# A token shift by one row: 112 + 15 + 1 rows of both halves in three transfers instead of 127 + 127 + 1

## The chip, the cores and the metric

The kernel runs on one core of a Trainium2 chip. Its time is the device time of one execution in microseconds (us). TensorE (PE) has two clock levels, 1.2 and 2.4 GHz, and the profile gives the granted clock as a share of the higher one.

## The reference

Two blocks of a transformer run one after the other on 256 tokens of width 1024, batch 1. The first block has two layers (windowed attention with a dense feed-forward, then attention with forgetting and a mixture of 8 experts). The second block mixes three branches: a recurrence of the RWKV-7 kind, a block attention and a state space model. A mixture of 32 experts follows. The change touches one step of the recurrence. Its input `z` is the projection of each token onto 1792 columns, and each token is blended with the token before it, the first token with zero:

```
z = x @ w_in[:, :1792]                    # 256 tokens x 1792
shifted = concat([zeros(1), z[:-1]])      # by one token
z = z + (shifted - z) * mu                # mu: one number per column
```

## The kernel before

Tokens lie on the 128 partitions in two halves, so `rz` is a tile of [128, 2, 1792]: partition p of half `tb` is token 128*tb + p. A shift by one token is a move by one partition, which compute engines don't do here; it is done with transfers from SBUF to SBUF into the tile `rzp`.

The projection is computed in four chunks of columns, in the order `ZCHUNKS = ((1536, 256), (512, 512), (0, 512), (1024, 512))`. For each, `gemm` multiplies for both halves, and each half's result is copied from PSUM to `rz` by ScalarE (ACT, L310) or VectorE (DVE, L312). Then `shift` is started for the chunk. Its first part clears row 0 of `rzp` on GpSimd (POOL, L1867), issues the transfers on SyncE (SP: L1869 twice, 127 rows of each half; L1870, the row that goes from the last token of the first half to the first row of the second), and loads the chunk's `mu` (tile `rmu`, L1883). Its second part (`tensor_sub`, POOL L1873 for half 0, DVE L1874 for half 1) and third part (L1877, L1878) stand in the program inside the next chunk's multiplications. Those of the last chunk stand inside the first gate's, `gate(2, m)`. The tile `rzp` has one buffer, so a chunk's transfers wait until the chunk before is blended.

Every engine works its own list in the order in which the program was recorded. `weave` recorded this order by an estimate of the time on PE, and it is the same in both kernels. So an instruction that waits holds all that stand behind it on its engine. SP issues the transfers above and also the weight loads: `wr` tiles (L107), each issued when a buffer is free, that is after a `wr` was split into high and low parts `ws` by ACT (L123) and DVE (L124). Then come the recurrence's constants: `rk_k`, `rk_a` and others, loaded by `begin` right behind the last chunk's `rmu`.

Names used below: the transposes through PE of `sq` (L222) belong to the state space branch, and their input is made by DVE L1790 and L1792. The transposes of `rz` (L222) begin the recurrence (`early`), after ACT L1914 and L1915. `early` then multiplies the keys by `rk_k` (DVE L1932) and takes exponentials (ACT L1942 to L1944). L2415 on DVE and L2416 on ACT are the gate's bias and sigmoid. Behind this stage follow the recurrence itself, the last projections, and the mixture of 32 experts, whose weights are loaded through the same `wr` buffers.

Of the kernel before, what the change touches and what calls it, by code (L numbers as in the profile page):

```python
# [1809 lines left out]
class Rwkv:  # L1810
# [51 lines left out]
    def shift(self, ep, c, w):  # L1862

        k, nc, z = self.k, self.k.nc, self.z
        cs = slice(c, c + w)
        zp = ep.tile([128, 2, 512], F32, name="rzp", tag="rzp", bufs=1)
        nc.gpsimd.memset(zp[0:1, 0, :w], 0.0)  # L1867
        for tb in range(2):
            nc.sync.dma_start(zp[1:128, tb, :w], z[0:127, tb, cs])  # L1869
        nc.sync.dma_start(zp[0:1, 1, :w], z[127:128, 0, cs])  # L1870
        mu = self.rowload(ep, "rwkv_mu_2", 512, "rmu", c)
        yield
        nc.gpsimd.tensor_sub(zp[:, 0, :w], zp[:, 0, :w], z[:, 0, cs])  # L1873
        nc.vector.tensor_sub(zp[:, 1, :w], zp[:, 1, :w], z[:, 1, cs])  # L1874
        yield
        for tb, e in ((1, nc.vector), (0, nc.gpsimd)):
            e.tensor_mul(zp[:, tb, :w], zp[:, tb, :w], mu[:, :w])  # L1877
            e.tensor_add(z[:, tb, cs], z[:, tb, cs], zp[:, tb, :w])  # L1878
# [934 lines left out]
```

## Time and profile before

| | |
|---|---|
| time, median of 3 runs (lowest to highest) | 1944.18 us (1944.09 to 1948.15) |
| the profiled execution's own time | 1946.39 us |
| its span, first to last instruction | 1944.7 us |
| PE busy | 1763.3 us, 91% |
| DVE, ACT, POOL busy | 709.1, 450.3, 375.5 us |
| mean granted clock | 0.958 |

The times in views count from the span's start. What lies around the span in the profiled execution is 1946.39 - 1944.7 = 1.7 us. A row of a timeline gives start, duration, engine, line, operation and tiles; in brackets the engine's idle time before it and what ended it. `SPq` rows are issues of transfers: their duration is the time that SP took to issue, not that of the transfer.

### The profile page before, as it was taken

The page shows a single profiled execution, that of the slowest core. Times are in us where ns is not written, and L with a number is a line of the kernel's source. Part 1 is how long each engine was busy: PE and PEld are TensorE (multiplying, and loading weights), DVE is VectorE, ACT ScalarE, POOL GpSimd, SP SyncE. Part 2 cuts the span into 40 slices and gives each one's busy share as a digit, 9 for nine tenths or more (in the row PEclk, how much of TensorE's full clock was granted, in tenths as well). Part 3 has the DMA queues.
Part 4 walks back from the last instruction along what each step waited for, and adds up shares of the span by engine and source line. Part 5 has one row for each costly group of instructions (what it writes and reads, how often), then busy time and mean ns, then how long its engine had stood idle before and what let it go on. Part 6 is the DMA issues. An engine that isn't in the chain of part 4 may idle for free. (4 is left out here: it accounts for less than half of the span.)

```text
span 1944.7 us, 41930 instructions
## 1 busy us (share of the span) xinstructions
PE 1763.3 (91%) x18587; PEld 1200.5 (62%) x18587; DVE 709.1 (36%) x1081; ACT 450.3 (23%) x785; POOL 375.5 (19%) x636
## 2 busy tenths in 40 slices
PE   8989999899699999999999999899637989889886
PEld 7867888797546555454545354588526767766552
DVE  5658655554401202020202020457517565621102
ACT  5534443353200000000000100043214333211101
POOL 5411999111100000000000000163114142000001
PEclk9999999899899999999999999899878999989998
DMA  6515665545399999999999799465224233899997
GB/s 217 161 63 186 215 213 194 158 120 215 127 388 386 385 398 376 410 369 408 375 405 379 284 422 423 154 210 164 85 83 153 78 93 121 315 355 408 409 408 302
DMA packets 138588, 515.99 MB, mean 265 GB/s; under 512 B 22248, under 2 KB 51350, under 8 KB 112800
## 3 DMA queue, kind: packets, MB, share of 16 engines
q1 hardware_dynamic: 135120, 497.39, 68.1%
q0 software_dynamic: 3280, 15.83, 2.4%
q8 instruction: 149, 2.44, 0.5%
q14 instruction: 39, 0.32, 0.1%
HBM read 503.48 MB, written 7.87 MB: 263 GB/s over the span
## 5 line engine op out<-in xcount | busy, mean ns | idle before, releaser
L218 PE MATMUL bank_r<-wl,gx 128*32 128x352 f32 x6144 | 462.2, 462 | 7.6 <-DMA wl<-in_w_exp_in_dram 5.2
L218 PE MATMUL bank_g<-ws,xh 128*128 128x256 f32 (+2 forms) x1440 | 388.4, 350 | 11.6 <-DVE ws L124 4.1
L218 PEld LDWEIGHTS bank_r<-wl,gx 128*32 128x32 f32 x6144 | 205.4, 111 | 257.9 <-issue 220.5
L124 DVE TENSOR_TENSOR ws<-wr,ws 128x1024 fp32r<-128x1024 f32 (+1 forms) x200 | 258.1, 1302 | 210.6 <-ACT ws L123 210.4
L218 PEld LDWEIGHTS bank_g<-ws,xh 128*128 128x128 f32 x1440 | 257.4, 195 | 50.5 <-issue 7.0
L123 ACT ACTIVATE ws<-wr 128x1024 fp32r<-128x1024 f32 (+1 forms) x200 | 209.3, 1057 | 171.6 <-PE bank_g L218 107.8
L218 PE MATMUL bank_g<-ws,xl 128*128 128x256 f32 (+2 forms) x720 | 235.9, 343 | 4.3 <-DVE xl L341 4.3
L218 PE MATMUL bank_r<-wl,ehT 128*32 128x256 f32 x4224 | 230.0, 379 | 1.7 <-DVE ehT L1400 1.5
L1399 DVE TENSOR_TENSOR eh<-eh,bank_r 128x352 f32<-128x352 f32 x48 | 22.9, 505 | 535.6 <-PE bank_r L218 535.1
L218 PEld LDWEIGHTS bank_r<-wl,ehT 128*32 128x32 f32 x4224 | 139.8, 110 | 91.0 <-issue 5.5
L533 POOL TENSOR_SCALAR lnmv<-lnmv 128x1 f32<-128x1 f32 x10 | 7.7, 771 | 823.7 <-DVE lnmv L532 823.7
L218 PEld LDWEIGHTS bank_g<-ws,xl 128*128 128x128 f32 x720 | 140.9, 196 | 18.9 <-DVE xl L341 5.8
L1420 ACT COPY ey<-bank_r 128x256 f32<-128x256 f32 x24 | 8.9, 372 | 456.7 <-PE bank_r L218 456.1
L218 PE MATMUL bank_g<-wr,xgx 128*32 128x256 f32 x864 | 65.6, 388 | 19.3 <-DMA wr<-in_expert_w_up_dram 7.0
L1391 ACT ACTIVATE eh<-bank_r 128x352 f32<-128x352 f32 x48 | 22.2, 464 | 206.7 <-PE bank_r L218 201.6
L218 PEld LDWEIGHTS bank_t<-xOH,x 128*128 128x128 f32 x256 | 61.7, 336 | 3.8 <-issue 2.9
L218 PE MATMUL bank_t<-xOH,x 128*128 128x128 f32 x256 | 63.2, 409 | 0.9 <-DVE xOH L2586 0.9
L218 PEld LDWEIGHTS bank_g<-wr,xgx 128*32 128x32 f32 x864 | 30.5, 111 | 53.9 <-DMA wr<-in_expert_w_up_dram 12.8
L615 POOL TENSOR_TENSOR aP<-aP,ast 128x512 f32<-128x512 f32 (+1 forms) x20 | 24.8, 1242 | 174.9 <-DVE ast L613 133.7
L218 PE MATMUL bank_g<-ws,hh 128*128 128x512 f32 x176 | 57.5, 399 | 0.0
L218 PE MATMUL bank_g<-ws,oh 128*128 128x512 f32 x128 | 44.6, 411 | 0.0
L1400 DVE STREAM_TRANSPOSE ehT<-eh 128x704 f32<-128x704 f32 x24 | 43.0, 1791 | 0.8
(698 smaller groups left out, 2102.0 us busy)
## 6 DMA issues: line engine op xcount, KB each, us to landing
wl<-in_w_exp_in_dram SPq DMA_DIRECT2D x128, 1408.0 KB, 9.0
wl<-in_w_exp_out_dram SPq DMA_DIRECT2D x64, 1408.0 KB, 8.9
wr<-in_expert_w_gate_dram SPq DMA_DIRECT2D x56, 512.0 KB, 10.2
wr<-in_w_in_dram SPq DMA_DIRECT2D x54, 512.0 KB, 4.1
wr<-in_expert_w_down_dram SPq DMA_DIRECT2D x54, 512.0 KB, 10.2
wr<-in_expert_w_up_dram SPq DMA_DIRECT2D x52, 512.0 KB, 10.2
wr<-in_w_ffn_in_dram SPq DMA_DIRECT2D x44, 512.0 KB, 4.1
wr<-in_w_out_dram SPq DMA_DIRECT2D x24, 512.0 KB, 4.4
```

Source lines behind the costliest of these rows:

```text
L123: nc.scalar.activation(hv, v, AF.Copy)
L124: nc.vector.tensor_sub(lv, v, hv.bitcast(F32))
L218: self.nc.tensor.matmul(out, lhsT, rhs, start=start, stop=stop)
L533: nc.gpsimd.tensor_scalar(mv[:, 2:3], mv[:, 1:2], 1e-5, None, op0=OP.add)
L615: e.tensor_mul(P[:, hs, :nk], P[:, hs, :nk], st[:, 3, hs].rearrange("p (h o) -> p h o", o=1).to_broadcast([128, 2, nk]))
L1391: nc.scalar.activation(h[:, g, s * H2:s * H2 + H2], pa[g][s], AF.Silu)
L1399: nc.vector.tensor_mul(v, v, pb[g][s])
L1400: nc.vector.transpose(hT[:, g], h[:, g].rearrange("p (r j) -> p j r", j=KF))
L1420: nc.scalar.copy(y[:, g], ps[g])
```

## The change

The two transfers of 127 rows, one for each half, become one of 112 rows of both halves and one of 15 rows of both halves. The single row stays as it is.

```
-        for tb in range(2):
-            nc.sync.dma_start(zp[1:128, tb, :w], z[0:127, tb, cs])
+        nc.sync.dma_start(zp[1:113, :, :w], z[0:112, :, cs])
+        nc.sync.dma_start(zp[113:128, :, :w], z[112:127, :, cs])
         nc.sync.dma_start(zp[0:1, 1, :w], z[127:128, 0, cs])
```

The lists of PE, DVE, ACT and POOL are the same in both programs. Only SP's differs, at four places. This is the third and fourth of them: the chunks of columns 0 and 1024. Each row is one issue; the numbers at its end are the pattern of the transfer (rows first), and x2 stands for two rows alike.

```order
 L107 DMA wr_13338<-in_w_in_dram 128x2x512
 L107 DMA wr_13361<-in_w_in_dram 128x2x512
-L1869 DMA rzp<-rz 127x512 x2
+L1868 DMA rzp<-rz 112x2x512
+L1869 DMA rzp<-rz 15x2x512
 L1870 DMA rzp<-rz 1x16x32
 L1883 DMA rmu<-in_rwkv_mu_dram 128x512
 L107 DMA wr_13437<-in_w_in_dram 128x2x512
 L107 DMA wr_13456<-in_w_in_dram 128x2x512
```

Two transfers by halves became two by rows, at the same place in SP's list; nothing moved past another load. Behind the last chunk's `rmu` SP's list goes on with the recurrence's constants, as before (rows of the changed program):

```order
 L1883 DMA rmu<-in_rwkv_mu_dram 128x512
 L1883 DMA rk_k<-in_rwkv_k_k_dram 128x512
 L1883 DMA rk_a<-in_rwkv_k_a_dram 128x512
 L1883 DMA rr_k<-in_rwkv_r_k_dram 128x512
 L1883 DMA rln_w<-in_rwkv_ln_w_dram 128x512
```

These rows moved against nothing: the single row's transfer and `rmu` stand ahead of them in both programs.

## Rows read from the trace of the kernel before

**Rows 1.** The page: span, then PE's busy tenths in 40 slices.
```profile
span 1944.7 us, 41930 instructions
...
PE   8989999899699999999999999899637989889886
```

**Rows 2.** PE's timeline, 1358 to 1475 us: its four rows with long idle time.
```profile
1363.65 1.22 PE L218 MATMUL bank_g<-ws,xh 128*128 128x512 f32 x2 [4.05 <-DVE ws L124]
...
1397.38 2.09 PE L222 MATMUL bank_t<-ident,sq 128*128 128x128 f32 x8 [14.22 <-DVE sq L1792]
...
1429.80 0.66 PE L222 MATMUL bank_t<-ident,rz 128*128 128x128 f32 x2 [15.95 <-DVE rz L312]
...
1467.44 1.87 PE L218 MATMUL bank_t<-rind,ru 128*128 128x2 f32 x8 [22.63 <-ACT ru L1943]
```

**Rows 3.** DVE's timeline, 1381 to 1464 us.
```profile
1381.50 1.23 DVE L124 TENSOR_TENSOR ws<-wr,ws 128x1024 fp32r<-128x1024 f32 x1 [1.65 <-ACT ws L123]
1393.46 0.69 DVE L1874 TENSOR_TENSOR rzp<-rzp,rz 128x512 f32<-128x512 f32 x1 [10.74 <-DMA rzp<-rz]
...
1397.15 0.41 DVE L1790 TENSOR_SCALAR st<-st 128x512 f32<-128x512 f32 x1
1397.60 0.69 DVE L1792 TENSOR_TENSOR sq<-hsv,st 128x512 f32<-128x512 f32 x1
...
1426.16 0.69 DVE L1874 TENSOR_TENSOR rzp<-rzp,rz 128x512 f32<-128x512 f32 x1 [18.11 <-DMA rzp<-rz]
...
1428.97 0.68 DVE L312 COPY rz<-bank_g 128x512 f32<-128x512 f32 x1
...
1458.60 1.18 DVE L1932 TENSOR_TENSOR ru<-rz,rk_k 128x512 f32<-128x512 f32 x1 [22.22 <-DMA rk_k<-in_rwkv_k_k_dram]
...
1463.65 0.68 DVE L2415 TENSOR_TENSOR hm<-bank_g,hgb 128x512 f32<-128x512 f32 x1
```

**Rows 4.** SP's timeline at the chunks of columns 512, 0 and 1024.
```profile
1367.39 5.50 SPq L1869 DMA_DIRECT2D rzp<-rz  x2
1372.93 10.17 SPq L1870 DMA_DIRECT2D rzp<-rz  x1
...
1401.42 4.83 SPq L1869 DMA_DIRECT2D rzp<-rz  x2
...
1431.52 6.16 SPq L1869 DMA_DIRECT2D rzp<-rz  x2
1437.73 10.30 SPq L1870 DMA_DIRECT2D rzp<-rz  x1
...
1448.70 0.42 SPq L1883 DMA_DIRECT2D rk_k<-in_rwkv_k_k_dram  x1
```

**Rows 5.** Stretches: length, busy us of PE to POOL, PE clock, DMA share, GB/s.
```profile
1363.60:1369.20 5.60, 5.55 (x34) 4.92 (x34) 4.82 (x7) 1.17 (x2) 1.09 (x2) 0.71 0.67 190
...
1397.30:1401.00 3.70, 3.62 (x13) 3.00 (x14) 3.63 (x6) 2.09 (x3) 0.00 (x0) 0.51 0.14 14
...
1429.80:1434.00 4.20, 4.20 (x10) 2.68 (x12) 4.17 (x5) 0.00 (x0) 1.50 (x3) 0.50 0.56 149
...
1441.50:1444.90 3.40, 3.30 (x11) 1.70 (x9) 0.00 (x0) 0.00 (x0) 0.00 (x0) 1.00 0.06 24
...
1467.40:1471.00 3.60, 3.56 (x12) 3.20 (x13) 0.00 (x0) 3.55 (x4) 1.55 (x2) 0.50 0.06 24
```

**Rows 6.** Issue to landing, min/median/max: `wr` from w_in, 1300 to 1480 us; `hgb`.
```profile
DMA to landing us min/median/max: 3.6/5.8/12.1
...
DMA to landing us min/median/max: 3.4/3.7/6.8
```

**Rows 7.** ACT's timeline around the first piece of `early`.
```profile
1414.17 0.31 ACT L1915 ACTIVATE rz<-rz 128x128 f32<-128x128 f32 x1
```

**Rows 8.** A stretch behind the stage, columns as in rows 5.
```profile
1590.00:1620.00 30.00, 30.00 (x489) 23.87 (x486) 15.46 (x20) 7.29 (x9) 9.33 (x8) 1.00 0.35 104
```

**Rows 9.** SP's own waits, 1640 to 1680 us: in total, times, longest.
```profile
SPq L107 <- DVE ws L124: 28.0, 12, 10.9
```

## The prediction

> **What bounds the kernel now.** I read the page's slices first. PE is busy at nine tenths or nearly so almost everywhere, but two slices next to each other, about 1361 to 1458 us, show 6 and 3 tenths, and the slice behind them 7 [rows 1]. That is where the four chunks are shifted. Next I read PE's timeline there. Four waits stand out: 4.05 us, 14.22, 15.95 and 22.63 [rows 2]. The first is not ended by a shift: DVE had other work ahead of the split of a weight. The other three make 52.8 us, and they are the change's field.
>
> Next I read DVE's timeline to see what held it [rows 3]. It sat idle 10.74 us and 18.11 us ahead of L1874, both ended by the landing of `rzp`, and 22.22 us ahead of L1932, ended by the landing of `rk_k`. Then SP: issuing the two half transfers took it 5.5 us and the single row 10.17 us in the chunk of columns 512, and 6.16 and 10.30 us in that of columns 1024. `rk_k`, which waits for no computed value, was issued only at 1448.70 [rows 4]. The stretches say why: from 1441.5 to 1444.9, with a half transfer under way, the DMA share is 0.06, one engine of 16, at 24 GB/s [rows 5]. A half of 127 rows of 2 KB is 260,096 bytes; at 24 GB/s that is 10.8 us, and two of them 21.7. This fits: the first issue at 1367.39 and DVE's start at 1393.46 lie 26.1 us apart [rows 3, 4]. So now the two halves go one after the other through a single DMA engine, and SP can't issue past them.
>
> **The change part by part.** Removed: eight transfers of 127 rows. Added: four of 112 rows and four of 15 rows, both halves in each. I expect the 112 rows to be spread over 16 engines, as 128 rows of a `wr` are. Nearest rows for the landing: `hgb`, 256 KB, 3.4 to 6.8 us (median 3.7), and the `wr`s of this stretch, 512 KB, 3.6 to 12.1 us (median 5.8), the long ones behind the half transfers [rows 6]. The 15 rows are 61,440 bytes, at one engine's 24 GB/s 2.6 us, and less on more engines. I take 5 us from a chunk's first issue to the last landing; bounds 3.4 and 12.1 + 2.6 = 14.7. SP's issues I take at 0.6 us each. One more issue per shift is then 0.6 us on SP, in time that SP spends waiting now: no cost. One wait is moved: the first transfer now needs both halves' copies. DVE's or ACT's second copy was there before the second issue anyway, and SP's list has nothing else between the two, so I cost that at nothing; should it matter, it is the few us by which the first half started earlier.
>
> The Trainium skill speaks to the spread ("DMA: Bandwidth & Descriptors", section "Why a DMA increments its semaphore by 16 and not by 1"): a transfer uses the largest number of engines up to 16 that divides the count of its slowest dimension, hence 1 for 127. By it 112 rows use 16 and 15 rows use 15. The trace agrees for 127 (share 0.06) [rows 5]; no run here shows the other two.
>
> First shift that counts, columns 512. PE stops at 1397.38 - 14.22 = 1383.16 [rows 2] for transposes of `sq`, whose input DVE makes behind L1874. DVE was free at 1381.50 + 1.23 = 1382.73 [rows 3]. In the new kernel SP issues from 1367.4 as before and the rows lie in `rzp` by 1372.4 (1382.1 at the upper bound), so DVE goes on at 1382.7. L1874 0.69, L1790 0.41, L1792 0.69 [rows 3] end at 1384.5. PE then waits 1.4 us instead of 14.2: 12.8 saved. What is late next is DVE's own work.
>
> Second, columns 0. All that follows is 12.8 us earlier. SP's first issue moves from 1401.42 to 1388.6 [rows 4], landing by 1393.6. DVE reaches L1874 at 1426.16 - 18.11 = 1408.05 before [rows 3], now at 1395.3: no wait. Behind it stand L1874, one split and the copy L312, 0.69 + 1.2 + 0.68, ready by 1398 or, if the split waits for ACT, 1399. PE has work until 1429.80 - 15.95 = 1413.85 before, now 1401.05, so L312 is no longer late. Next in line is ACT: the transposes also read what L1915 writes, at 1414.48 before [rows 7], now 1401.7. I leave 1 us of 15.95: 15.0 saved, 27.8 in all.
>
> Third, columns 1024 and the constants. SP's first issue moves from 1431.52 to 1403.7 [rows 4]. Three issues and `rmu` at 0.6 us, then `rk_k` goes out at about 1406.2 and lands 3.7 to 5.8 us later, say at 1411.5. DVE is ready for L1932 at 1458.60 - 22.22 - 27.8 = 1408.6, so it waits 3 us and not 22. L1932 0.7, two splits of 1.2 and L1874 0.7 follow; L2415 starts at 1415.3. From L2415 to PE's next matmul it took 1467.44 - 1463.65 = 3.8 us (a sigmoid, a table load and two exponentials on ACT) [rows 2, 3]: 1419.1. PE runs out of work at 1467.44 - 22.63 - 27.8 = 1417.0. It waits 2 us instead of 22.6: 20.6 saved.
>
> The waits give 12.8 + 15.0 + 20.6 = 48.4 us. Then the clock. After each of the three waits PE ran at the lower level, 1.2 GHz: granted 0.51 over 3.7 us, 0.50 over 4.2, 0.50 over 3.6 [rows 5]. Work at half the rate for that long loses 0.49 x 3.7 + 0.5 x 4.2 + 0.5 x 3.6 = 5.7 us. After the 4.05 us wait the clock fell too (0.71 over 5.6 us) [rows 5]; no row shows what waits of 1 or 2 us do. Bounds 0 and 5.7; I take 4, since two of the three leftovers are under 1.5 us.
>
> Sum 52.4. Is it kept to the end? Behind the stage PE is the bound again (30.00 busy of 30 us) [rows 8], and the experts' weight loads start as splits free buffers: SP waits there for DVE L124, 28.0 us in 12 waits [rows 9]. So the DMA-bound end starts earlier by the same amount. Against the profiled execution's 1946.39 us (span 1944.7 [rows 1] and 1.7 around it) that is 1894.0. The median lies 2.2 us lower, at 1944.18: **1892 us**.
>
> **The rivals.**
> - The single row is slow by itself: its 10.2 us on SP [rows 4] stay. For: the row itself doesn't change. Against: it ends when the first half must have gone through. At columns 512 the delay is covered. At columns 0 the row would land at 1388.6 + 1.2 + 10.2 + 3 = 1403.0, 7.7 us after DVE comes to it; L312 is late by some 4 us. At columns 1024 `rk_k` goes out about 14 us later than above with what came before, and after the 3 us wait that DVE has anyway, PE is late by 9 to 10. Together 13 us back: about 1905.
> - The spread doesn't come: 112 rows too go through one engine, or the two transfers gain nothing over one another. For: nothing in the trace shows 112 rows. Against: 128-row loads run at many times 24 GB/s (190 GB/s in a stretch that `wr`s share) [rows 5]. Bytes and engine would be the same, so the time too: 1944. The Trainium skill ("DMA: Bandwidth & Descriptors", section "Rules for kernel authors") holds that two transfers to disjoint sets of partitions only serialize and aren't worth making; taken alone that would be this case. The trace disagrees as far as it goes: with share 0.06 the halves don't fill 16 engines [rows 5].
> - Another late thing takes over half of the room, for instance the splits `ws` on DVE, which go on while PE waits now and would then have to keep up: half of 52.4 gained, 1918. For: the first wait of the four is such a one, 4.05 us [rows 2]. Against: DVE is itself idle for 51 us of the three waits' time [rows 3].
> - Slower: rows of two separate runs are cut into short pieces. The single row is a pattern of 16 pieces. If 112 x 2 rows were cut alike, 3,584 pieces would lie on 16 engines, 224 on each, against 254 packets on one engine now; a piece that took as long as a 2 KB packet does (2,048 bytes at 24 GB/s, 0.085 us) would give 19 us per shift, as now. It decides against the change where a piece takes longer than that, or is half as long: 38 us, 16 more in each of three waits, 1992. Against it: a `wr` has the same pattern, 128 x 2 x 512, and lands in 3.6 us at best [rows 6].
>
> **How the numbers follow.** Forecast as worked out 0.80, the slow single row 0.07, half the room 0.06, no spread 0.05, slower 0.02. Low end: all 52.8 us of waits and all 5.7 of the clock: 1944.2 - 58.5 = 1885.7, so 1885. High end: landings of 14.7 us, which come 8 us too late at columns 0 and so cost much as the slow single row does (1905), and most of the clock's 4 us not given back: 1908. A measurement of this kernel can tell about 0.2%, 3.9 us, from no change; faster 0.93, same 0.05, slower 0.02.
>
> **What would show it.** In the profile after: SP's issues at L1868 to L1870 under 1 us each; no `rzp` wait of more than 2 us ahead of L1874 on DVE; the 112 rows landed within 3 to 6 us; `rk_k` issued some 42 us earlier (1406 for 1448.70); PE's waits at the three places 1 to 3 us; a granted clock near 1.0 behind the first two. I am wrong if SP still takes 10 us at L1870, if DVE still waits for `rzp`, or if these waits vanish and PE stops as long for a weight split or ACT's tables. If the stage shortens by 50 us and the kernel doesn't, the end of the kernel was bound by loads that don't move with it.

## The result and the profile after

The changed kernel takes 1899.49 us (median of 4 runs, 1898.93 to 1900.47), the kernel before beside it on the same chip 1946.16 (4 runs, 1944.09 to 1949.74). The ratio is 0.9754, with a 95% interval of 0.974 to 0.9767: 46.7 us or 2.46% faster. The forecast was 1892 in a range of 1885 to 1908. The profiled execution of the changed kernel took 1900.47 us, of which the span is 1898.8.

The page of the changed kernel: span, then busy time of each engine with its share, then PE's busy tenths in 40 slices.

```profile
span 1898.8 us, 41933 instructions
...
PE 1764.5 (93%) x18587; PEld 1201.4 (63%) x18587; DVE 704.4 (37%) x1081; ACT 451.0 (24%) x785; POOL 372.5 (20%) x636
...
PE   8989999899799999999999989989989898899886
```

The 6, 3 and 7 that stood in the middle of PE's row [rows 1] are gone; the row shows no hole there now. In PE's timeline of the changed kernel, 1358 to 1440 us, these are the rows that answer to [rows 2]:

```profile
1364.84 1.22 PE L218 MATMUL bank_g<-ws,xh 128*128 128x512 f32 x2 [4.04 <-DVE ws L124]
...
1386.58 0.63 PE L222 MATMUL bank_t<-ident,sq 128*128 128x128 f32 x4 [2.21 <-DVE sq L1792]
1387.55 0.66 PE L222 MATMUL bank_t<-ident,sq 128*128 128x128 f32 x4 [0.34 <-DVE sq L1792]
...
1404.13 0.33 PE L222 MATMUL bank_t<-ident,rz 128*128 128x128 f32 x1 [0.57 <-ACT rz L1915]
...
1420.95 1.87 PE L218 MATMUL bank_t<-rind,ru 128*128 128x2 f32 x8 [4.41 <-ACT ru L1943]
```

The wait of 4 us that no shift ended is still there. The three behind it went from 14.22, 15.95 and 22.63 us to 2.55 (in two pieces), 0.57 and 4.41. From the first of these rows to the last I measure the length of the stage, which all experiments below are compared by. Before, it was 1467.44 - 1363.65 = 103.79 us [rows 2]; now it is 1420.95 - 1364.84 = 56.11, which is 47.68 shorter. Ahead of it the changed kernel is 1.19 us later (1364.84 for 1363.65), and behind it 0.6 longer (1898.8 - 1420.95 = 477.85 for 1944.7 - 1467.44 = 477.26). 47.68 - 1.19 - 0.59 is 45.9, the whole difference of the two profiled executions (1946.39 - 1900.47). So the gain comes out of this stage alone, and the end of the kernel keeps it.

SP's timeline of the changed kernel, at the chunks of columns 512 and 1024, answers to [rows 4]:

```profile
1368.64 0.66 SPq L1868 DMA_DIRECT2D rzp<-rz  x1
1369.35 0.91 SPq L1869 DMA_DIRECT2D rzp<-rz  x1
1370.31 1.51 SPq L1870 DMA_DIRECT2D rzp<-rz  x1
1371.87 0.58 SPq L1883 DMA_DIRECT2D rmu<-in_rwkv_mu_dram  x1
...
1403.65 0.65 SPq L1868 DMA_DIRECT2D rzp<-rz  x1
...
1406.80 0.43 SPq L1883 DMA_DIRECT2D rk_k<-in_rwkv_k_k_dram  x1
```

The single row, on which SP sat for 10.17 us, now takes it 1.51, and `rk_k` goes out 42 us earlier (1406.80 for 1448.70). The view of the tile `rzp` in the changed kernel gives the time from issue to landing:

```profile
DMA to landing us min/median/max: 2.5/4.6/7.9
```

DVE's timeline of the changed kernel answers to [rows 3]:

```profile
1377.72 2.05 DVE L124 TENSOR_TENSOR ws<-wr,ws 128x1024 fp32r<-128x1024 f32 x1 [3.49 <-ACT ws L123]
...
1383.54 1.23 DVE L124 TENSOR_TENSOR ws<-wr,ws 128x1024 fp32r<-128x1024 f32 x1 [1.65 <-ACT ws L123]
1384.68 0.69 DVE L1874 TENSOR_TENSOR rzp<-rzp,rz 128x512 f32<-128x512 f32 x1
...
1397.56 1.80 DVE L1874 TENSOR_TENSOR rzp<-rzp,rz 128x512 f32<-128x512 f32 x1
1399.29 2.31 DVE L124 TENSOR_TENSOR ws<-wr,ws 128x1024 fp32r<-128x1024 f32 x1
1401.52 0.68 DVE L312 COPY rz<-bank_g 128x512 f32<-128x512 f32 x1
...
1412.66 1.71 DVE L1932 TENSOR_TENSOR ru<-rz,rk_k 128x512 f32<-128x512 f32 x1 [4.42 <-DMA rk_k<-in_rwkv_k_k_dram]
...
1417.16 0.68 DVE L2415 TENSOR_TENSOR hm<-bank_g,hgb 128x512 f32<-128x512 f32 x1
```

L1874 no longer waits at all, where it waited 10.74 and 18.11 us; what is left is 4.42 us for `rk_k`. Last, stretches of the changed kernel, columns as in [rows 5]: just behind SP's first issue at the chunk of columns 512, then behind the first wait (three rows), behind the second, and behind the third.

```profile
1369.00:1371.00 2.00, 2.00 (x18) 1.78 (x17) 0.92 (x2) 0.00 (x0) 0.15 (x1) 1.00 0.92 317
1386.60:1388.50 1.90, 1.55 (x10) 1.24 (x11) 1.87 (x3) 0.84 (x2) 0.00 (x0) 1.00 0.62 235
1388.50:1392.00 3.50, 3.50 (x10) 2.71 (x9) 3.46 (x7) 1.28 (x2) 0.52 (x1) 0.51 0.50 152
1392.00:1404.10 12.10, 11.56 (x52) 9.26 (x50) 9.76 (x9) 6.49 (x9) 4.66 (x4) 1.00 0.50 133
1404.10:1416.50 12.40, 12.37 (x47) 8.10 (x47) 7.25 (x9) 4.75 (x6) 4.51 (x5) 1.00 0.89 262
...
1420.90:1426.10 5.20, 5.15 (x16) 4.47 (x17) 0.30 (x1) 4.81 (x6) 1.57 (x2) 0.50 0.15 47
```

With the 112 rows under way the DMA share is 0.92, where it was 0.06 with a half of 127 rows; weight loads may have their part in the 0.92. The lower level of the clock (0.5 of full speed) still comes behind the first and the third wait, for 3.5 and 5.2 us; behind the first it comes 1.9 us after PE has resumed. Behind the second, of 0.57 us, it doesn't come: the granted clock is 1.00 there, where it was 0.50.

### The profile page after: what moved, and what is told of

It is laid out like the page before. It is cut to its first block, busy times and chain, and to the rows that moved or that the text cites. A ratio compares the mean times of both kernels' runs of the same rounds, so it can differ in the third digit from the quotient of the medians.

```text
span 1898.8 us, 41933 instructions
## 1 busy us (share of the span) xinstructions
PE 1764.5 (93%) x18587; PEld 1201.4 (63%) x18587; DVE 704.4 (37%) x1081; ACT 451.0 (24%) x785; POOL 372.5 (20%) x636
## 5 line engine op out<-in xcount | busy, mean ns | idle before, releaser
L124 DVE TENSOR_TENSOR ws<-wr,ws 128x1024 fp32r<-128x1024 f32 (+1 forms) x200 | 256.2, 1292 | 211.3 <-ACT ws L123 211.0
## 6 DMA issues: line engine op xcount, KB each, us to landing
wr<-in_expert_w_gate_dram SPq DMA_DIRECT2D x56, 512.0 KB, 10.2
wr<-in_expert_w_down_dram SPq DMA_DIRECT2D x54, 512.0 KB, 10.2
wr<-in_expert_w_up_dram SPq DMA_DIRECT2D x52, 512.0 KB, 10.2
```

The source lines that it names most:

```text
L124: nc.vector.tensor_sub(lv, v, hv.bitcast(F32))
```

## The experiments

**The theory.** Two transfers of 127 rows each went through one DMA engine, one behind the other, and SP could not issue past them; 112 and 15 rows are spread over many engines. **The rivals.** It could be the merging of the halves that helps. It could be the single row that is slow. Or the count of the rows may not matter, only the splitting into a large and a small piece. All diffs below are against the changed kernel; the lines for the 112 and the 15 rows, which they replace, are shown once. The kernel before ran beside each group; its medians were 1947.62, 1947.92 and 1948.34 us. "Stage" is the length defined above: 103.8 before, 56.1 after, and 54.9 in a second profile of the changed kernel.

**Merged, not split.** One transfer of 127 rows of both halves.

```
-        nc.sync.dma_start(zp[1:113, :, :w], z[0:112, :, cs])
-        nc.sync.dma_start(zp[113:128, :, :w], z[112:127, :, cs])
+        nc.sync.dma_start(zp[1:128, :, :w], z[0:127, :, cs])
```

> 127 rows of both halves in one transfer, then the single row: the halves are merged as in the change, but the count of rows stays 127. Theory (a transfer of 127 rows runs on one DMA engine, and the change helps because 112 and 15 rows don't): 254 packets on one engine, some 21 us per shift as before; time 1940 to 1955 us, DVE's waits for rzp and rk_k as before. Rival (it is the merging of the halves, or one transfer fewer on SP, that helps): about 1900 us.

Measured: 1952.27 us, ratio 1.0024 (1.0013 to 1.0035); stage 107.75; PE's three waits 15.74, 16.35 and 23.56 us. The merging alone gains nothing: it is some 5 us slower than the kernel before beside it. SP's timeline in this kernel, chunk of columns 512:

```profile
1370.09 0.75 SPq L1868 DMA_DIRECT2D rzp<-rz  x1
1370.89 14.71 SPq L1869 DMA_DIRECT2D rzp<-rz  x1
1385.66 0.58 SPq L1882 DMA_DIRECT2D rmu<-in_rwkv_mu_dram  x1
```

With both halves in one transfer, it is the next issue, that of the single row, on which SP is held, for 14.7 us.

**Split, not merged.** 112 and 15 rows of each half by itself, five transfers per shift.

```
+        for tb in range(2):
+            nc.sync.dma_start(zp[1:113, tb, :w], z[0:112, tb, cs])
+            nc.sync.dma_start(zp[113:128, tb, :w], z[112:127, tb, cs])
```

> 112 and 15 rows, but of each half by itself: five transfers per shift, nothing merged. Theory (the count of rows decides): as the changed kernel plus two more issues of 0.7 to 0.9 us per shift, of which the last shift's reach rk_k: 1899 to 1904 us. Rival (merging helps): about 1946 us.

Measured: 1901.95 us, ratio 0.9774 (0.9752 to 0.9795); stage 57.43; waits 3.79, 0.57 and 4.64 us. The gain is in the split by rows. The two more issues per shift show on SP, where `rk_k` went out at 1409.33 instead of 1406.80; but the stage is only 1.3 us longer than that of the changed kernel, whose own two profiles differ by as much (56.1 and 54.9), so what the merging is worth can't be told from nothing.

**One row more.** 113, 14 and 1 rows.

```
+        nc.sync.dma_start(zp[1:114, :, :w], z[0:113, :, cs])
+        nc.sync.dma_start(zp[114:128, :, :w], z[113:127, :, cs])
```

> 113 + 14 + 1 rows, both halves, in place of 112 + 15 + 1: one row moved from one transfer to the other. Theory, in the form that a transfer is spread over as many engines, up to 16, as divide its count of rows: 113 is prime, so 226 packets on one engine, 18.5 us; DVE waits 7 to 16 us for rzp again, 1935 to 1950 us. Rival (any split into a large and a small piece spreads): within 2 us of the changed kernel, about 1900. The Trainium skill, DMA: Bandwidth & Descriptors, section Why a DMA increments its semaphore by 16 and not by 1, has the rule of the largest divisor; by it this is one engine.

Measured: 1946.42 us, ratio 0.9992 (0.998 to 1.0005); stage 100.71. The whole gain in time is gone, for one row moved from one transfer to the other. In the profile of this kernel, PE's first wait, and then a stretch while the large piece of the last chunk is under way:

```profile
1397.08 2.09 PE L222 MATMUL bank_t<-ident,sq 128*128 128x128 f32 x8 [13.01 <-DVE sq L1792]
```

```profile
1435.00:1443.00 8.00, 8.00 (x31) 5.35 (x29) 0.00 (x0) 3.02 (x4) 0.00 (x0) 1.00 0.06 24
```

A DMA share of 0.06 at 24 GB/s again: 113 rows go through one engine. SP's second issue, the piece of 14 rows, took 12.07 us. So it is the count that decides, not that there is a large and a small piece.

**A count in between.** 122, 5 and 1 rows.

```
+        nc.sync.dma_start(zp[1:123, :, :w], z[0:122, :, cs])
+        nc.sync.dma_start(zp[123:128, :, :w], z[122:127, :, cs])
```

> 122 + 5 + 1 rows, both halves. 122 is 2 x 61. Theory in the divisor form: two engines, 122 packets on each, 10 us, about half of what one engine took; hidden at the chunk of columns 512, some 6 us late at columns 0, and rk_k some 5 to 10 us later at the last: 1908 to 1922 us, between the two kernels. If such a transfer falls to one engine: 1940 or more; if it is spread evenly over 16: 1900.

Measured: 1919.19 us, ratio 0.9854 (0.983 to 0.9878); stage 75.14. Three views of this kernel: PE's timeline, a stretch while the 122 rows of the chunk of columns 512 are under way, and POOL's L1873 there, which waits for the shifted rows:

```profile
1388.55 2.08 PE L222 MATMUL bank_t<-ident,sq 128*128 128x128 f32 x8 [4.48 <-DVE sq L1792]
...
1411.57 0.66 PE L222 MATMUL bank_t<-ident,rz 128*128 128x128 f32 x2 [6.79 <-DVE rz L312]
...
1439.76 1.86 PE L218 MATMUL bank_t<-rind,ru 128*128 128x2 f32 x8 [13.82 <-ACT ru L1943]
```

```profile
1374.00:1375.00 1.00, 1.00 (x12) 1.00 (x11) 0.00 (x0) 0.00 (x0) 0.00 (x0) 1.00 0.13 47
```

```profile
1382.99 1.79 POOL L1873 TENSOR_TENSOR rzp<-rzp,rz 128x512 f32<-128x512 f32 x1 [14.07 <-DMA rzp<-rz]
```

The waits lie between those of before and after; I had expected the delay at columns 512 to be hidden, but it cost PE 4.48 us. A DMA share of 0.13 is two engines of 16, at 47 GB/s. The time until the rows are there fits this. From SP's first issue at the chunk of columns 512 to the start of POOL's L1873 (L1872 in the merged kernel) it takes 26.4 us with 127 rows merged, 23.7 with 113, 14.6 with 122 (1382.99 - 1368.41) and 5.5 with 112. Bytes over engines at 24 GB/s each make 21.7 and 19.3 us on one engine for 127 and 113 rows, 10.4 on two for 122 (499,712 bytes) and, if they use 16, 1.2 for 112 (estimates): in each case 4.2 to 4.7 us less. The rule of the Trainium skill that the prediction cites ("DMA: Bandwidth & Descriptors", section "Why a DMA increments its semaphore by 16 and not by 1") gives 16 engines for 112, one for 113 and two for 122. The runs agree with it for 113 and 122 by the DMA share, 0.06 and 0.13; for 112 they show a wide spread, not the number 16.

**A count that is no multiple of 16.** 126, 1 and 1 rows.

```
+        nc.sync.dma_start(zp[1:127, :, :w], z[0:126, :, cs])
+        nc.sync.dma_start(zp[127:128, :, :w], z[126:127, :, cs])
```

> 126 + 1 + 1 rows, both halves in the first two: one row fewer than the kernel before has in a transfer. 126 is 9 x 14. Theory in the divisor form: 14 engines, 18 packets of 2 KB on each, 1.5 us against 1.2 for the 112 rows; 1898 to 1903 us. Rival (only counts that are a multiple of 16 are spread): one engine, 252 packets, 1940 or more.

Measured: 1900.52 us, ratio 0.975 (0.9724 to 0.9776); stage 55.29. 126 rows do as well as 112 (from the first issue to POOL's L1873 it takes 5.5 us too), so neither a smaller piece nor the number 16 is needed, only a count that divides well.

**The single row first.** The kernel before, with the single row issued ahead of the halves of 127 rows.

```
         nc.sync.dma_start(zp[0:1, 1, :w], z[127:128, 0, cs])
+        for tb in range(2):
+            nc.sync.dma_start(zp[1:128, tb, :w], z[0:127, tb, cs])
```

> The kernel before with the single row issued ahead of the two transfers of 127 rows. Theory (SP is held by what the half transfers still owe to their one engine, not by the row): the row's issue takes under 1 us in its new place, and the hold of some 10 us moves to rmu's issue, which is now third; time 1943 to 1950 us. Rival of the prediction (the single row is slow by itself): the row takes 8 to 10 us first in line too.

Measured: 1948.57 us, ratio 0.9997 (0.9983 to 1.001). SP's timeline in this kernel, chunk of columns 512:

```profile
1368.22 0.55 SPq L1868 DMA_DIRECT2D rzp<-rz  x1
1368.82 4.78 SPq L1870 DMA_DIRECT2D rzp<-rz  x2
1373.64 10.16 SPq L1883 DMA_DIRECT2D rmu<-in_rwkv_mu_dram  x1
```

The row takes 0.55 us when nothing lies ahead of it, and the 10 us fall on `rmu`, which now stands behind the two halves and is a load of 128 rows. The row is not slow; what stands there, the row or `rmu`, is held. The rival of the slow single row falls.

**Another queue.** The halves of 127 rows as before, issued by GpSimd instead of SP.

```
+        for tb in range(2):
+            nc.gpsimd.dma_start(zp[1:128, tb, :w], z[0:127, tb, cs])
```

> The kernel before with the two transfers of 127 rows issued from GpSimd's queue in place of SyncE's; the rest stays on SyncE. If a transfer of 127 rows is confined to one engine on whichever queue: SP is no longer held, so the constants come early and the third wait goes (some 18 us), but rzp lands late as before: 1920 to 1935 us. If that queue spreads it over all engines: 1898 to 1908 us.

Measured: 1896.92 us, ratio 0.9745 (0.9722 to 0.9768); stage 54.30; waits 1.71, 0.26 and 4.23 us: just under the 1898 to 1908 expected if that queue spreads the rows. The view of the transfers, first in this kernel (halves of 127 rows, 254 KB, median us to landing at the end), then in the changed one (112 rows of both halves):

```profile
rzp<-rz POOLq DMA_DIRECT2D x6, 254.0 KB, 5.2
```

```profile
rzp<-rz SPq DMA_DIRECT2D x3, 448.0 KB, 4.6
```

From this queue halves of 127 rows land about as fast as 112 rows of both halves from SP's, and far under the 10.8 us that a half takes on one engine at 24 GB/s. So 127 is a bad count on SP's queue, not on every one. The same section of the Trainium skill names such an exception, for some direct copies that GpSimd issues, and the run agrees.

**Each shift by itself.** The change for the chunk of columns 512 alone (`if c == 512:`, else the two transfers of 127 rows), and for that of columns 1024 alone.

> The change at the chunk of columns 512 alone; the other three shifts as before. Theory (three waits in a row, each worth its own leftover): PE's first wait of 14.2 us goes down to 2 to 3 us, the other two stay: 1946 less 11 to 14, that is 1932 to 1936 us. Rival (the waits make up for one another: what the first gives is given back at the second): 1943 to 1947 us.

> The change at the last chunk (columns 1024) alone. Theory: the first two waits of PE stay, the third of 22.6 us goes down to 3 to 6 us since rk_k goes out some 15 us earlier: 1946 less 17 to 21, that is 1925 to 1930 us. With the chunk of columns 512 alone and the same sum for columns 0 (15 us) this must come to the whole change's 46.7. Rival (the constants are late for another reason, their buffers or their own transfers): 1940 or more.

Measured for columns 512: 1938.45 us, ratio 0.9942 (0.9921 to 0.9963), stage 92.47, so 11.3 shorter; waits 2.84, 15.66 and 23.92. For columns 1024: 1931.08 us, ratio 0.9907 (0.9886 to 0.9929), stage 84.80, 19.0 shorter; waits 13.78, 15.70 and 3.92. Both medians are 1 to 2.5 us above the ranges expected. The kernel before beside them was 1.9 us above the 1946 that I reckoned from, but the medians fell by only 9.5 and 16.8 us where 11 to 14 and 17 to 21 were expected; the stages shortened by the size expected. The waits don't make up for one another: taking one away leaves the other two within about 1.3 us of what they were. The chunk of columns 0 wasn't run alone, so that the three gains add up is not shown; what is left for it is 47.7 - 11.3 - 19.0 = 17.4 us of the stage, and its wait of 15.95 us fell by 15.4.

**What is left: `rk_k`.** In the changed kernel DVE still waits 4.42 us for `rk_k`, issued behind the last shift. Here the constants (issued in `begin`) go out ahead of that shift.

```
                     late = r.shift(ep, c, n)
-                    next(late)
+                    if c != ZCHUNKS[-1][0]:
+                        next(late)
...
             r.begin(rw.enter_context(k.pool(name="rw", bufs=1)))
+            next(lates[0])
```

> The changed kernel, with the recurrence's constants (rk_k and the four behind it) issued ahead of the last chunk's shift instead of behind it. Theory (what is left of the third wait, 4.4 us on PE, is rk_k's late issue and landing): rk_k goes out some 4 us earlier and lands by 1407 us in place of 1412.5; DVE doesn't wait at L1932, and PE's third wait falls to 1 to 2 us, with less time at the lower clock behind it: 2 to 6 us faster than the changed kernel, 1894 to 1898 us. Rival (the last shift is then as late as the constants were, and DVE waits at L1874): within 1 us of the changed kernel.

Measured: 1901.28 us, ratio 0.9765 (0.9746 to 0.9784), and the changed kernel again beside it:

> The changed kernel once more, on the chip of the two others: 1897 to 1903 us.

Measured: 1896.61 us (5 runs, 1894.73 to 1900.59), ratio 0.9742 (0.9722 to 0.9762), 0.4 us below the range expected. So the earlier constants gain nothing, and my theory of 2 to 6 us fell. DVE's timeline with the constants first:

```profile
1408.36 1.64 DVE L1874 TENSOR_TENSOR rzp<-rzp,rz 128x512 f32<-128x512 f32 x1 [3.22 <-DMA rzp<-rz]
```

The wait for `rk_k` is gone, and one for the shift stands in its place; PE's third wait is 5.34 us, and the stage 55.24, as long as that of the changed kernel beside it (54.9). The two share a queue, and here the one behind was late, whichever it was. Then both at once: constants first, and the halves from GpSimd (this diff and that of the other queue together).

> The constants ahead of the last shift as in the run above, and the halves of 127 rows issued from GpSimd's queue, which left SyncE free and spread them. If both gains add: 1890 to 1895 us. If the queue from GpSimd gave nothing of its own: as the run with the constants first.

Measured: 1897.87 us (5 runs, 1894.21 to 1898.77), ratio 0.9741 (0.9721 to 0.9761). The stage is 51.78 us, 3.2 shorter than that of the changed kernel beside it, and PE's third wait 2.57; but the total is not told from 1896.61. I expected 1890 to 1895, which was missed; why 3 us of the stage don't show in the total is open. No version that I ran is measurably faster than the changed kernel.

## Why the prediction was right

The mechanism held in each part. Two transfers through one engine were what held SP and DVE (113 rows: no gain; 127 merged: no gain); 112 and 15 rows are spread; each of the three waits fell, and those of the two shifts run alone fell without the others; and the end of the kernel kept what the stage gave. The forecast sum was 52.4 us, and the stage gave 47.7. That is 4.7 of the 6.5 us by which the profiled execution is longer than forecast (1900.47 for 1894.0); the other 1.8 lie ahead of the stage and behind it. The terms, as the prediction put them:

| term | forecast, us | measured, us |
|---|---|---|
| wait 1, columns 512 | 14.2 to 1.4: 12.8 | 14.22 to 2.55: 11.7 |
| wait 2, columns 0 | 15.95 to 1: 15.0 | 15.95 to 0.57: 15.4 |
| wait 3, columns 1024 and constants | 22.6 to 2: 20.6 | 22.63 to 4.41: 18.2 |
| clock | 4 | 2.4, with all that isn't a wait (47.7 - 45.3) |
| sum | 52.4 | 47.7 |

**Wait 1.** What is late next is DVE's own work, as forecast. But it is later by the 0.8 us that one split of a weight took longer: 2.05 us where a split of that form took 1.23 [rows 3]. The second piece of the wait, 0.34 us, is DVE's L1790 and L1792 for the second half, which the prediction left out. The long split lies beside POOL's work on the shifted rows, which now comes that early. POOL's timeline of the changed kernel:

```profile
1376.02 1.29 POOL L1877 TENSOR_TENSOR rzp<-rzp,rmu 128x512 f32<-128x512 f32 x1 [0.62 <-DMA rmu<-in_rwkv_mu_dram]
1377.39 1.29 POOL L1878 TENSOR_TENSOR rz<-rz,rzp 128x512 f32<-128x512 f32 x1
...
1412.53 1.29 POOL L1878 TENSOR_TENSOR rz<-rz,rzp 128x512 f32<-128x512 f32 x1
```

The split began at 1377.72, 0.96 us ahead of the end of POOL's second row. That the one slows the other was not tried by itself; the rows only lie side by side, here, at columns 0 (L1874 1.80 us, L124 2.31) and at L1932. The kernel before has such rows too, DVE's first and POOL's below:

```profile
1394.07 1.49 DVE L1790 TENSOR_SCALAR st<-st 128x512 f32<-128x512 f32 x1
1395.60 1.63 DVE L1792 TENSOR_TENSOR sq<-hsv,st 128x512 f32<-128x512 f32 x1
```

```profile
1381.69 2.17 POOL L1873 TENSOR_TENSOR rzp<-rzp,rz 128x512 f32<-128x512 f32 x1 [13.74 <-DMA rzp<-rz]
1393.96 1.32 POOL L1877 TENSOR_TENSOR rzp<-rzp,rmu 128x512 f32<-128x512 f32 x1 [10.09 <-DMA rmu<-in_rwkv_mu_dram]
1395.36 1.32 POOL L1878 TENSOR_TENSOR rz<-rz,rzp 128x512 f32<-128x512 f32 x1
```

The same L1790 and L1792 took 0.41 and 0.69 us for the second half [rows 3], which the prediction took. At 1381.69 it was POOL's row that was long, and DVE's split beside it took its 1.23 us [rows 3].

**Wait 2.** As forecast, and ended by ACT's L1915, which the prediction named as next in line. That DVE's L312 was not late was nearer than forecast: it ended at 1402.20, 1.4 us before PE ran out of work at 1403.56, where the forecast left 2 to 3, for L1874 and the split ahead of it took 1.80 and 2.31 us and not 0.69 and 1.2. In part this is luck.

**Wait 3** is the mis-sized one. `rk_k` went out at 1406.80 for the forecast 1406.2, and L1932, which waited for it, started at 1412.66: nearly 5.9 us, the far end of the 3.7 to 5.8 that the prediction gave, where it took 5.3. L1932 itself took 1.71 us, where the prediction wrote 0.7; the row of before says 1.18 [rows 3], so this was misread by 0.5, and the other 0.5 lies beside POOL's row at 1412.53. From L2415 to PE's matmul it is 1420.95 - 1417.16 = 3.79 us, as forecast. L1932 began 1.2 us later than forecast, from there to L2415 it took 4.5 us for 3.8, and PE ran out of work 0.5 us earlier (1416.54): that is the difference.

**The clock.** The prediction wanted a granted clock near 1.0 behind the first two places, because their waits would be short. Behind the second it is so; behind the first it was 0.51 over 3.5 us, though the wait was only 2.55. Behind the third it stayed at the lower level for 5.2 us. The 5.7 us that the prediction counted as lost were too few: its stretches of 4.2 and 3.6 us [rows 5] end before the lower level does. In the kernel before it lasted 5.3 us behind the second wait and 5.2 behind the third:

```profile
1429.80:1435.10 5.30, 5.30 (x13) 2.72 (x13) 4.24 (x6) 0.00 (x0) 1.50 (x3) 0.50 0.57 150
1467.40:1472.60 5.20, 5.16 (x16) 4.49 (x17) 0.32 (x1) 4.79 (x6) 1.57 (x2) 0.50 0.12 43
```

So the loss before was 0.49 x 3.7 + 0.5 x 5.3 + 0.5 x 5.2 = 7.1 us, and 0.49 x 3.5 + 0.5 x 5.2 = 4.3 of it are left. 2.7 or 2.8 came back, nearly all behind the second wait, where 4 were forecast; this is about the 2.4 of the table. The term was too large because the lower level still came behind the first and the third wait, at full length.

**The rivals.** No spread: shown wrong by the change, and shown to be what happens at 113. The slow single row: shown wrong by issuing it first. Another late thing taking half: didn't come. Pieces cut short: didn't come; the 112 rows of 512 columns landed in 4.6 us at the median. Of the signs, SP's issues shown above are under 1 us but for one of 1.51; the landings of all transfers of `rzp` lay between 2.5 and 7.9 us where 3 to 6 was said of the 112 rows (the 7.9 is the 112 rows of the first chunk, of 256 columns); no wait for `rzp` is left on DVE; PE's waits are 2.55, 0.57 and 4.41 us where 1 to 3 was said.

**A rule and a measurement that differ.** The rule in the Trainium skill that two transfers to disjoint halves of the partitions only serialize ("DMA: Bandwidth & Descriptors", section "Rules for kernel authors"), which the prediction weighs for disjoint sets, doesn't hold for the counts of this case: 127 rows in one transfer took 1952.27 us (ratio 1.0024) and 112 + 15 in two 1899.49 (0.9754). The rule takes it that both transfers use all 16 engines; 127 rows used one.

## What to carry to other kernels

When a shift or a copy moves 127 rows (or 113, or, less badly, 122) from one partition to the next, look at the DMA share of a stretch in which it is under way: 0.06 means one engine of 16. Cut the count into pieces that divide well (112 + 15, or 126 + 1), or issue it from GpSimd's queue, and look at what the same queue issues next: here the longest wait was for `rk_k`, a load that needed nothing computed and could not go out. Then size the gain by each wait's own successor, not by the transfer's time.

## What the runs showed of the hardware

- An issue on SP can be held by transfers that are confined to one engine or two: 10.2 us for the third in line behind two halves of 127 rows (a single row, or `rmu` of 128 rows), 14.7 us for the second behind one merged transfer, 12.07 behind 113 rows and 3.4 behind 122; behind 112 rows the second issue took 0.9. What sets the length of such a hold was not tried.
- One row decides: 112 rows of both halves, 1899.49 us; 113, 1946.42; 122, 1919.19; 126, 1900.52; 127, 1952.27. GpSimd's queue spreads 127 rows: 1896.92.
- One engine moved 24 GB/s at a DMA share of 0.06, and 122 rows showed a share of 0.13. From the first issue to the start of the instruction that waits for the rows it took some 4 to 5 us more than the estimate of bytes over engines, from 112 rows (5.5 us) to 127 merged (26.4).
- The granted clock fell to 0.51 for 3.5 us behind a wait in two pieces of 2.21 and 0.34 us, 1.9 us after PE had resumed, and stayed at 1.00 behind one of 0.57 us. Behind waits of 4.41, 15.95 and 22.63 us it stood at 0.50 for 5.2 to 5.3 us alike, behind one of 14.22 for 3.5.
- DVE's instructions often took longer where POOL's lay beside them: 2.05 and 2.31 us for 1.23 (L124), 1.80 for 0.69 (L1874), 1.49 for 0.41 (L1790). Once it was POOL's that was long, 2.17 us for 1.27 (L1873). This was not tried by itself.
